# First conditioning rows of a two-layer encoder: plain fp32 products, or split operands in two fp32r passes

## The chip, the cores and the metric

The kernel runs on one core of one Trainium2 chip. The metric is the device time of one execution in microseconds (us). Single executions vary, so the time of a kernel is the median of several runs; beside it stands one execution recorded by the hardware profiler.

A core has TensorE (matmul; its weight loads are listed apart), VectorE, ScalarE, GpSimd and SyncE. SyncE's queue (SP) issues the transfers between DRAM and on-chip memory. Matmuls write into eight PSUM banks of 128 x 512 fp32.

## The reference

A trunk of two layers, for a prompt of 2048 frames and 32 sample frames, width 1024. Each layer scales and shifts its normalised input by rows that come from a conditioning vector:

```python
def ada_norm(x, c, g, w_ada, b_ada):
    mod = jax.nn.silu(c) @ w_ada + b_ada
    shift, scale, gate = jnp.split(mod[:, None, :], 3, axis=-1)
    return rms_norm(x, g) * (1 + scale) + shift, gate

for i in range(DEPTH):
    h_p, gate_p = ada_norm(y_p, c_prompt, norm_g[i], ada_w[i], ada_b[i])
    h_s, gate_s = ada_norm(y_s, c_sample, norm_g[i], ada_w[i], ada_b[i])
    # layer 0: chunk-band attention with a relative bias; layer 1: latent attention
    ...
    y_p = y_p + gate_p * out_p
    y_s = y_s + gate_s * out_s
```

`c` is a vector of 1024 for the prompt and one for the sample; `w_ada` is 1024 x 3072 fp32. The case concerns `shift` and `scale` of layer 0, the first two thirds of `mod`, for both vectors.

## The kernel before

The kernel opens with a prelude: constants, then the conditioning rows of layer 0 (`ada`), then the bias tables and the first 512 frames. Layer 0 follows in 32 steps (two halves, eight pairs of heads, two blocks of 512 frames), then its output projection with the inputs of layer 1, the latent attention, and the end. Nearly all large products run as "split" products: an operand is written as a high part in fp32r and a low part (the rest, also fp32r), and three fp32r matmuls take the place of one in plain fp32. A kernel-wide helper makes the parts: `halve` (L146) casts the raw fp32 tile to the high part on ScalarE (L148) and subtracts that from the raw tile in place on VectorE or GpSimd (L149). `twin` gives a second name with the other type to the same place in memory.

**The conditioning rows before.** `cT` holds silu(c) for both vectors, as eight pieces of 128 x 2. `ada(0, (0, 1), pre[0:11])` (L377) works through two pairs: pair 0 is `shift`, pair 1 `scale`, each 1024 columns. `pre` is a list of sixteen places of 128 x 1024 fp32, which later hold the h tiles `HT0` and `HT1`; in the profile the first eight are called `HT_@1` and the others `HT_@5`. Two places take the bias rows, one takes the finished rows, and a ring of eight takes weight rows. `ada_part` (L272) loads, for each of the eight values of k, 128 rows of `ada_w` (512 KB), and multiplies `cT[:, k]` with their two halves of 512 columns in plain fp32 (L278). VectorE then adds the bias (L282), TensorE turns each piece of 128 columns into a column by a transpose (L291), and VectorE writes `sc` (shift, L298) or `gc` (1 + scale, times the norm's gain, L300).

A weight row can be loaded into a place when the matmuls of the row before it there are done. All transfers are issued from SP's queue (L104), in an order that a scheduler fixes when the program is built: an instruction that is not ready in its reckoning is passed by others. Each engine then runs its queue strictly in order.

**The other conditioning rows** (the gate of layer 0, all of layer 1) are computed during the steps, in `ada_piece` (L304). They use `cH` (L229), where c stands as high part in columns 0 and 1 and low part in columns 2 and 3, and weights split by `halve`; a matmul with the high and one with the low half of the weights (L320) give four rows. `fold` (L232), three identity matrices of 2 x 2 below each other, adds the high rows, the low rows and the bias rows, and turns them to columns at once (L336).

**What comes next in the prelude.** The bias table of layer 0 is loaded, extended by VectorE (L386, L388) and written to DRAM twice (`ext`, `rext`). `make_h` (L415) loads x for 128 frames, takes the mean square on ScalarE in two halves (L344; the squares themselves go to a PSUM bank that nobody reads), normalises (L348), transposes (L428), applies `gc` and `sc` on ScalarE (L432) and splits the result into `HT0` (L435, L436). The banks of tag `tp` and `mx` are three in this part, used in turn by the transposes of `ada` and by these squares. `fetch_w` and `split_w` load and split the projection weights (`wr` to `wq`, casts at L458), and `project` multiplies (L189 to L191, the three matmuls of a split product).

Of the kernel before, what the change touches and what calls it, by code (L numbers as in the profile page):

```python
# [11 lines left out]
ALU = mybir.AluOpType  # L12
# [4 lines left out]
D = 1024  # L17
SEQ = 2048
NS = 32
KT = D // 128  # L20
# [11 lines left out]
def f32(ap):  # L32
    return ap if ap.dtype == F32 else ap.bitcast(F32)
# [49 lines left out]
def located(nc, name, n, dtype, col):  # L83
    t = nc.alloc_sbuf_tensor_at(f"{name}@{len(PLACES)}", [128, n], dtype, offset=BASE + 4 * col).ap()
    PLACES[t.tensor.name] = name, n, dtype, col
    return t


def twin(nc, ap):

    name, n, dtype, col = PLACES[ap.tensor.name]
    key = ap.tensor.name, "twin"
    if key not in PLACES:
        t = PLACES[key] = located(nc, name + "_", n, F32R if dtype == F32 else F32, col)
        PLACES[t.tensor.name, "twin"] = ap
    return bass.AP(PLACES[key].tensor, ap.offset, [list(x) for x in ap.ap])
# [3 lines left out]
def trunk(ctx: ExitStack, tc: tile.TileContext, I, O, stop=99):  # L100
    nc = tc.nc
    V, S, G, T = nc.vector, nc.scalar, nc.gpsimd, nc.tensor
    def dma(dst, src, eng=nc.sync):
        eng.dma_start(f32(dst), f32(src))  # L104
# [21 lines left out]
    ident = const.tile([128, 128], F32, name="ident")  # L126
# [9 lines left out]
    def slot():  # L136
        return wp.tile([128, 2, 512], F32R, tag="w", name="w", bufs=wn)
# [8 lines left out]
    def halve(hi, raw, eng=None):  # L146

        S.copy(hi, raw)  # L148
        (eng or V).tensor_tensor(twin(nc, raw), raw, f32(hi), ALU.subtract)  # L149
# [43 lines left out]
    def bank(tag):  # L193
        order = psum[tag if tag in psum else "mx"]
        order.append(order.pop(0))
        return banks[order[-1]]
# [22 lines left out]
    cT = const.tile([128, KT, 2], F32, name="cT")  # L219
# [9 lines left out]
    cH = const.tile([128, KT, 4], F32R, name="cH")  # L229
    V.tensor_copy(cH[:, :, 0:2], cT)  # L230
    V.tensor_tensor(cH[:, :, 2:4], cT, f32(cH[:, :, 0:2]), ALU.subtract)
    fold = const.tile([6, 2], F32, name="fold")  # L232
# [3 lines left out]
    gate_d = [dram.tile([2, D], F32, name=f"gate{i}") for i in range(2)]  # L236
    gcol, scol = [], []

    def ada(i, parts, ring=None):

        if 0 in parts:
            ada_cols(i)
        gc, sc, gn = gcol[i], scol[i], gnorm[i]

        def row():
            if ring is None:
                return f32(slot()).rearrange("p a b -> p (a b)")
            ring.append(ring.pop(0))
            return ring[-1]

        bias_rows = []
        for pair in parts:
            bias_rows.append(row()[0:2, :])
            dma(bias_rows[-1], bass.AP(I["ada_b"].tensor, I["ada_b"].offset + (3 * i + pair) * D, [[0, 2], [1, D]]))
        modr = row()[0:2, :]
        if ring is not None:
            ring = ring[0:-len(parts) - 1]
        for pair, b in zip(parts, bias_rows):
            ada_part(i, pair, row, gc, sc, gn, b, modr)

    gnorm = []

    def ada_cols(i):
        gn = const.tile([128, KT], F32, name=f"gn{i}")
        dma(gn, I["norm_g"][i].rearrange("(k p) -> p k", p=128))
        gc = const.tile([128, KT, 2], F32, name=f"gc{i}")
        sc = const.tile([128, KT, 2], F32, name=f"sc{i}")
        gcol.append(gc)
        scol.append(sc)
        gnorm.append(gn)  # L270

    def ada_part(i, pair, row, gc, sc, gn, adab, modr):  # L272
        acc = [bank("mm") for _ in range(2)]
        for k in range(KT):
            w = row()
            dma(w, I["ada_w"][i, 128 * k:128 * k + 128, 1024 * pair:1024 * pair + 1024])
            for n in range(2):
                T.matmul(acc[n][0:2, :], cT[:, k, :], w[:, 512 * n:512 * n + 512],  # L278
                         start=(k == 0), stop=(k == KT - 1))
        for n in range(2):  # L280
            mr = modr[:, 512 * n:512 * n + 512]
            V.tensor_tensor(mr, acc[n][0:2, :], adab[:, 512 * n:512 * n + 512], ALU.add)  # L282
            ada_use(i, pair, n, mr)

    def ada_use(i, pair, n, mr):
        if pair == 2:
            dma(gate_d[i][:, 512 * n:512 * n + 512], mr)
            return
        tp = bank("tp")
        for q in range(4):  # L290
            T.transpose(tp[:, 2 * q:2 * q + 2], mr[:, 128 * q:128 * q + 128], ident[0:2, 0:2])  # L291
        ada_cols_use(i, pair, n, tp)

    def ada_cols_use(i, pair, n, tp):
        src = tp[:, 0:8].rearrange("p (k c) -> p k c", c=2)
        ks = slice(4 * n, 4 * n + 4)
        if pair == 0:
            V.tensor_copy(scol[i][:, ks, :], src)  # L298
        else:
            V.scalar_tensor_tensor(gcol[i][:, ks, :], src, 1.0,  # L300
                                   gnorm[i][:, ks].unsqueeze(2).broadcast_to([128, 4, 2]),
                                   ALU.add, ALU.mult)

    def ada_piece(i, pair, n, a, ws, rows):  # L304


        c0 = 1024 * pair + 512 * n
        if a == 0:
            dma(rows[4:6, :], bass.AP(I["ada_b"].tensor, I["ada_b"].offset + 3 * i * D + c0, [[0, 2], [1, 512]]))
        for k in range(2):  # L310
            r0 = 256 * a + 128 * k
            dma(twin(nc, ws[k][1]), I["ada_w"][i, r0:r0 + 128, c0:c0 + 512])
        yield
        for k in range(2):
            halve(ws[k][0], twin(nc, ws[k][1]), G)
        yield
        acc = bank("ad")[0:4, :]
        for k in range(2):
            for x in range(2):
                T.matmul(acc, cH[:, 2 * a + k, :], ws[k][x], start=(k == 0 and x == 0), stop=(k == 1 and x == 1))  # L320
        if a == 0:
            V.tensor_copy(rows[0:4, :], acc)
        else:
            V.tensor_tensor(rows[0:4, :], acc, rows[0:4, :], ALU.add)
        if a < 3:
            return
        if pair == 2:
            out = bank("ad")[0:2, :]
            T.matmul(out, fold, rows, start=True, stop=True)
            t = at1([128, 4, 128], "hs").rearrange("p j t -> p (j t)")[0:2, :]  # L330
            V.tensor_copy(t, out)
            dma(gate_d[i][:, c0 - 2048:c0 - 1536], t)
            return
        tp = bank("tp")
        for q in range(4):
            T.matmul(tp[:, 2 * q:2 * q + 2], rows[:, 128 * q:128 * q + 128], fold, start=True, stop=True)  # L336
        ada_cols_use(i, pair, n, tp)

    def xnorm(x, rows=128):

# [30 lines left out]
    def at1(shape, name, dt=F32, bufs=1):  # L371
        return at.tile(shape, dt, tag=name, name=name, bufs=bufs)


    pre = [twin(nc, at1([128, KT, 1024], f"HT{b}", F32R)) for b in range(2)]
    pre = [t[:, i, :] for t in pre for i in range(KT)]
    ada(0, (0, 1), pre[0:11])  # L377

# [31 lines left out]
    def xraw():  # L412
        return at1([128, D], "xr", bufs=2)
# [555 lines left out]
    for si, s in enumerate(steps):  # L969
# [21 lines left out]
        if si == ADA0:  # L991
            ada_cols(1)
            ring = [[twin(nc, t)[:, 512 * n:512 * n + 512] for n in range(2)] for t in (xraw(), xraw())]
            rows = twin(nc, hsT).rearrange("p k t -> p (k t)")[0:6, :]
            pieces = [ada_piece(i, pair, n, a, ring, rows) for i, pair in ((0, 2), (1, 0), (1, 1), (1, 2))
                      for n in range(2) for a in range(4)]
# [28 lines left out]
        for i, (h, n, c, t) in enumerate(items):  # L1025
# [3 lines left out]
            if len(fifo) > LAGA:  # L1029
                x = fifo.pop(0)  # L1030
# [139 lines left out]
    for t in range(17):  # L1170
        if t < 16:
            for n in range(2):
                out_tile(W, ready[t], n, gp)
            x = ready[t][0]
# [51 lines left out]
    def et(shape, name, dt=F32, bufs=1):  # L1226
        return ep.tile(shape, dt, tag=name, name=name, bufs=bufs)
# [531 lines left out]
    for i in range(len(items) + LAG + 20):  # L1759
# [12 lines left out]
        if i >= LAG and fifo:  # L1772
            u, t, p = fifo.pop(0)
            values(u, t, p)
            if t == u["order"][-1]:
                evac(u)
                later.append((i + DEN, denom, u))
                if u["blk"] % 2 and u["hd"] % 2:
                    n, u0 = INV if u["hd"] < 15 else (7, 9, 10, 10, 11), units[u["i"] - 1]
# [3 lines left out]
        while later and later[0][0] <= i:  # L1783
            _, f, u = later.pop(0)
            f(u)
        if i >= 100 and i % 25 == 0 and wload:
            k, n = wload.pop(0)
# [144 lines left out]
    def row(name):  # L1932
        return et([NS, D], name)
# [62 lines left out]
```

## Time and profile before

| | us |
|---|---|
| median of 3 runs | 3744.6 |
| lowest, highest | 3741.33, 3757.91 |
| the profiled execution | 3754.29 |
| its span in the trace | 3752.5 |

| engine | busy us | share of the span |
|---|---|---|
| TensorE (PE) | 3511.9 | 94% |
| VectorE (DVE) | 2914.7 | 78% |
| ScalarE (ACT) | 2173.0 | 58% |
| GpSimd (POOL) | 1681.1 | 45% |

All moments below are microseconds from the start of the span. Matmul ends are modelled, and matmuls are pipelined, so a matmul's own duration is longer than the distance to the next one; the pace is read from starts. Register, semaphore and transfer-issuing instructions are not counted as busy. The granted clock is TensorE's, as a share of 2.4 GHz.

### The profile page before, as it was taken

The numbers are of one execution on the slowest core, as the hardware profiler recorded it, in microseconds if no ns is written. First come the engines' busy times: TensorE is split into PE (matmuls) and PEld (weight loads), VectorE is DVE, ScalarE is ACT, GpSimd is POOL, SyncE is SP. The second block draws the span as 40 slices with busy tenths as digits, with TensorE's granted clock in tenths as the row PEclk, the third lists the DMA queues.
The fourth block names the chain that finished last, engine by engine and source line by source line (L and its number), as shares of the span: only waits on it lengthen the run. The fifth ranks groups of instructions, "written<-read, shape, count | busy, mean of one in ns | idle before, by whom it ended". The sixth has DMA issues, their size and how long they took to land. (4 is left out here: it accounts for less than half of the span.)

```text
span 3752.5 us, 57503 instructions
## 1 busy us (share of the span) xinstructions
PE 3511.9 (94%) x17834; PEld 2871.1 (77%) x17834; DVE 2914.7 (78%) x6716; ACT 2173.0 (58%) x5302; POOL 1681.1 (45%) x1744
## 2 busy tenths in 40 slices
PE   7899999989999999899989999888999999998999
PEld 4778877867777777677878888767777787777887
DVE  4788888888888888776776766788888888885653
ACT  3556555676666666542223655556776677775542
POOL 0122222344544444340012444458888888884032
PEclk9899999999999999699999999979999999999999
DMA  5222222222333333363444666563233233223253
GB/s 175 69 60 59 69 62 75 81 76 82 99 96 92 96 92 96 96 190 126 132 152 149 181 203 185 171 186 90 74 84 98 67 93 92 68 77 111 89 189 118
DMA packets 441984, 412.91 MB, mean 110 GB/s; under 512 B 68820, under 2 KB 364296, under 8 KB 434636
## 3 DMA queue, kind: packets, MB, share of 16 engines
q1 hardware_dynamic: 441676, 409.23, 37.3%
q8 instruction: 141, 2.31, 0.3%
q14 instruction: 167, 1.37, 0.1%
HBM read 251.72 MB, written 140.10 MB: 104 GB/s over the span
## 5 line engine op out<-in xcount | busy, mean ns | idle before, releaser
L1544 DVE TENSOR_REDUCE mp@325_17580<-bank 128x1 f32<-128x512 f32 (+3 forms) x384 | 233.8, 615 | 28.3 <-PE bank L1543 26.3
L675 ACT ACTIVATE bank<-bank 128x512 f32<-128x512 f32 x448 | 200.3, 447 | 0.0
L678 POOL TENSOR_TENSOR acc@61_865<-acc@61_865,P@63_893 128x256 f32<-128x256 f32 (+3 forms) x64 | 52.9, 826 | 172.4 <-ACT P@63_893 L673 143.3
L1544 DVE TENSOR_REDUCE mp@326_17581<-bank 128x1 f32<-128x512 f32 (+1 forms) x192 | 116.9, 613 | 16.7 <-PE bank L1543 16.0
L1577 ACT ACTIVATE P@436_22812<-bank 128x512 f32<-128x512 f32 (+2 forms) x156 | 83.3, 534 | 74.3 <-issue 38.6
L1577 ACT ACTIVATE P@438_22814<-bank 128x512 f32<-128x512 f32 (+2 forms) x156 | 83.2, 534 | 67.3 <-issue 35.7
L718 DVE RECIPROCAL ez@69_1265<-ez@69_1265 128x128 f32<-128x128 f32 x128 | 117.6, 926 | 0.0
L1577 ACT ACTIVATE P@437_22813<-bank 128x512 f32<-128x512 f32 (+2 forms) x156 | 83.5, 535 | 55.3 <-PE bank L1570 11.3
L1577 ACT ACTIVATE P@435_22811<-bank 128x512 f32<-128x512 f32 (+2 forms) x156 | 83.4, 535 | 54.3 <-issue 13.0
L678 POOL TENSOR_TENSOR acc@61_865<-acc@61_865,P@64_894 128x256 f32<-128x256 f32 (+3 forms) x64 | 53.2, 831 | 114.9 <-ACT P@64_894 L673 92.4
L678 POOL TENSOR_TENSOR acc@62_866<-acc@62_866,P@65_895 128x256 f32<-128x256 f32 (+3 forms) x64 | 53.9, 841 | 106.3 <-ACT P@65_895 L673 103.0
L678 POOL TENSOR_TENSOR acc@62_866<-acc@62_866,P@63_893 128x128 f32<-128x128 f32 (+3 forms) x64 | 54.1, 846 | 103.1 <-ACT P@63_893 L673 96.0
L673 ACT ACTIVATE P@64_894<-bank 128x256 f32<-128x256 f32 (+3 forms) x128 | 52.3, 409 | 76.9 <-DVE bank L667 42.1
L678 POOL TENSOR_TENSOR acc@61_865<-acc@61_865,P@65_895 128x128 f32<-128x128 f32 (+3 forms) x64 | 53.6, 838 | 95.3 <-ACT P@65_895 L673 77.5
L673 ACT ACTIVATE P@63_893<-bank 128x384 f32<-128x384 f32 (+3 forms) x128 | 52.6, 411 | 75.1 <-DVE bank L667 42.7
L673 ACT ACTIVATE P@65_895<-bank 128x128 f32<-128x128 f32 (+3 forms) x128 | 52.4, 409 | 75.0 <-DVE bank L667 44.3
L678 POOL TENSOR_TENSOR acc@62_866<-acc@62_866,P@64_894 128x256 f32<-128x256 f32 (+3 forms) x64 | 54.4, 850 | 86.9 <-ACT P@64_894 L673 84.9
L149 POOL TENSOR_TENSOR ozl@175_14851<-ozl_@180_14859,ozh@173_14849 128x1024 fp32r<-128x1024 f32 x8 | 19.3, 2412 | 151.0 <-ACT ozh@173_14849 L148 151.0
L676 DVE TENSOR_TENSOR Pl@58_862<-bank,Ph@55_859 128x512 fp32r<-128x512 f32 (+3 forms) x150 | 71.3, 475 | 18.1 <-ACT bank L675 16.4
L676 DVE TENSOR_TENSOR Pl@60_864<-bank,Ph@57_861 128x384 fp32r<-128x384 f32 (+3 forms) x149 | 71.7, 481 | 11.6 <-ACT bank L675 9.3
L676 DVE TENSOR_TENSOR Pl@59_863<-bank,Ph@56_860 128x384 fp32r<-128x384 f32 (+3 forms) x149 | 72.7, 488 | 8.3 <-ACT bank L675 5.8
L1594 DVE TENSOR_TENSOR bank<-bank,P@437_22813 128x512 f32<-128x512 f32 (+2 forms) x108 | 66.5, 616 | 12.8 <-ACT P@437_22813 L1577 12.0
(2154 smaller groups left out, 14849.6 us busy)
## 6 DMA issues: line engine op xcount, KB each, us to landing
h<-hT@203_14883 SPq DMA_DIRECT2D x16, 1024.0 KB
N<-hl@389_17976 SPq DMA_DIRECT2D x32, 512.0 KB
N<-hl@390_17977 SPq DMA_DIRECT2D x32, 512.0 KB
wr@10_296<-in_a_w_in SPq DMA_DIRECT2D x64, 192.0 KB
wr@11_297<-in_a_w_in SPq DMA_DIRECT2D x64, 192.0 KB
xr@9_231<-in_ada_w SPq DMA_DIRECT2D x32, 256.0 KB
xr@8_230<-in_ada_w SPq DMA_DIRECT2D x32, 256.0 KB
h1@220_14902<-h SPq DMA_DIRECT2D x8, 1024.0 KB
```

The source lines that it names most:

```text
L149: (eng or V).tensor_tensor(twin(nc, raw), raw, f32(hi), ALU.subtract)
L673: S.activation(P[:, 0:w], st[:, 0:w], AF.Exp)
L675: S.activation(st[:, 0:w], st[:, 0:w], AF.Exp)
L676: V.tensor_tensor(Pl[:, 0:w], st[:, 0:w], f32(Ph[:, 0:w]), ALU.subtract)
L678: G.tensor_tensor(u["acc"][:, qs], u["acc"][:, qs], P[:, 0:w], ALU.add)
L718: V.reciprocal(ez[:, cs], ez[:, cs])
L1544: V.tensor_reduce(mp[:, j, c:c + 1] if blk else m4[:, j:j + 1], X[:, 0:w], AX.X, ALU.max)
L1577: S.activation(P[:, 0:w], st[:, 0:w], AF.Exp)
L1594: V.tensor_tensor((u["acc"] if last else u["sum"])[:, qs], old, P[:, 0:w], ALU.add)
```

## The change

The first conditioning rows are computed in the manner of `ada_piece`, but by whole weight rows:

- `cH` takes the place of `cT` as the stationary operand, so a product has four rows.
- Ten places of `pre` are used, not eleven. Two hold the rows of the two pairs (four product rows and two bias rows each); the other eight are four pairs of places, one for the high and one for the low part of a weight row. The raw row is loaded into the low part's place.
- `halve` casts each 128 x 1024 row on ScalarE and subtracts on VectorE.
- For each half of 512 columns TensorE multiplies with the high and with the low part, in fp32r: four matmuls for each row in place of two plain fp32 products.
- The PSUM rows are copied by VectorE, and `fold` adds the six rows and turns them to columns.
- The bias rows of a pair are loaded at the start of that pair; before, both were loaded ahead of all weight rows.

`ada_use` is now shared by both ways. Nothing else of the program is changed.

```diff
-    def ada(i, parts, ring=None):
...
+    def ada(i, parts, ring):
+
+        ada_cols(i)
+        places = [(twin(nc, ring[2 + 2 * j]), twin(nc, ring[3 + 2 * j])) for j in range(4)]
         for pair in parts:
-            bias_rows.append(row()[0:2, :])
-            dma(bias_rows[-1], bass.AP(I["ada_b"].tensor, I["ada_b"].offset + (3 * i + pair) * D, [[0, 2], [1, D]]))
-        modr = row()[0:2, :]
-        if ring is not None:
-            ring = ring[0:-len(parts) - 1]
-        for pair, b in zip(parts, bias_rows):
-            ada_part(i, pair, row, gc, sc, gn, b, modr)
+            rows = ring[pair][0:6, :]
+            dma(rows[4:6, :], bass.AP(I["ada_b"].tensor, I["ada_b"].offset + (3 * i + pair) * D, [[0, 2], [1, D]]))
+            acc = [bank("mm")[0:4, :] for _ in range(2)]
+            for k in range(KT):
+                hi, lo = places[(KT * parts.index(pair) + k) % 4]
+                dma(twin(nc, lo), I["ada_w"][i, 128 * k:128 * k + 128, 1024 * pair:1024 * pair + 1024])
+                halve(hi, twin(nc, lo))
+                for n in range(2):
+                    for x in (hi, lo):
+                        T.matmul(acc[n], cH[:, k, :], x[:, 512 * n:512 * n + 512], start=(k == 0 and x is hi),
+                                 stop=(k == KT - 1 and x is lo))
+            for n in range(2):
+                half = rows[:, 512 * n:512 * n + 512]
+                V.tensor_copy(half[0:4, :], acc[n])
+                ada_use(i, pair, n, half)
...
-    def ada_part(i, pair, row, gc, sc, gn, adab, modr):
-        acc = [bank("mm") for _ in range(2)]
-        for k in range(KT):
-            w = row()
-            dma(w, I["ada_w"][i, 128 * k:128 * k + 128, 1024 * pair:1024 * pair + 1024])
-            for n in range(2):
-                T.matmul(acc[n][0:2, :], cT[:, k, :], w[:, 512 * n:512 * n + 512],
-                         start=(k == 0), stop=(k == KT - 1))
-        for n in range(2):
-            mr = modr[:, 512 * n:512 * n + 512]
-            V.tensor_tensor(mr, acc[n][0:2, :], adab[:, 512 * n:512 * n + 512], ALU.add)
-            ada_use(i, pair, n, mr)
...
+    def ada_use(i, pair, n, rows):
+
         tp = bank("tp")
         for q in range(4):
-            T.transpose(tp[:, 2 * q:2 * q + 2], mr[:, 128 * q:128 * q + 128], ident[0:2, 0:2])
-        ada_cols_use(i, pair, n, tp)
...
+            T.matmul(tp[:, 2 * q:2 * q + 2], rows[:, 128 * q:128 * q + 128], fold, start=True, stop=True)
...
-    ada(0, (0, 1), pre[0:11])
+    ada(0, (0, 1), pre[0:10])
```

## Rows read from the trace of the kernel before

**Rows 1.** The page's first part: busy us, share of the span and instructions of each engine.

```profile
PE 3511.9 (94%) x17834; PEld 2871.1 (77%) x17834; DVE 2914.7 (78%) x6716; ACT 2173.0 (58%) x5302; POOL 1681.1 (45%) x1744
```

**Rows 2.** Busy time of each engine in three stretches, and a heading line.

```profile
core 0: us, PE busy (x) PEld busy (x) DVE busy (x) ACT busy (x) POOL busy (x), PEclk, DMA share, GB/s
7.30:39.30 32.00, 31.50 (x80) 6.71 (x80) 4.48 (x11) 1.07 (x3) 0.00 (x0) 1.00 0.86 313
39.30:48.30 9.00, 3.41 (x18) 2.79 (x17) 7.58 (x31) 7.96 (x30) 0.00 (x0) 0.81 0.60 160
65.00:1400.00 1335.00, 1254.73 (x6486) 1026.08 (x6487) 1106.14 (x2903) 841.67 (x2124) 479.21 (x507) 0.98 0.28 78
```

**Rows 3.** Line L278: durations in ns (min/median/max), first and last start, shapes.

```profile
L278 PE MATMUL bank<-HT_@1_125,cT x40: 591/592/1061, 7.4 to 32.4; 128*2 128x512 f32 x40
...
L278 PE MATMUL bank<-HT_@5_127,cT x24: 592/592/592, 18.2 to 37.5; 128*2 128x512 f32 x24
```

**Rows 4.** Timeline of the weight loads: start, duration, form, idle before and what ended it.

```profile
9.01 0.13 PEld L278 LDWEIGHTS bank<-HT_@1_125,cT 128*2 128x2 f32 x1 [0.72 <-issue]
...
16.47 0.09 PEld L278 LDWEIGHTS bank<-HT_@1_125,cT 128*2 128x2 f32 x1 [0.34 <-issue]
```

**Rows 5.** SP's queue in the timeline (issue of transfers), and a stretch at full rate.

```profile
3.43 0.84 SPq L104 DMA_DIRECT2D HT_@1_125<-in_ada_w  x2
4.32 1.96 SPq L104 DMA_DIRECT2D fold<-ident  x3
...
23.52 0.33 SPq L104 DMA_DIRECT2D HT_@5_127<-in_ada_w  x1
23.95 0.38 SPq L104 DMA_DIRECT2D HT_@5_127<-in_a_rel_bias  x1
...
30.73 0.42 SPq L104 DMA_DIRECT2D xr@8_230<-in_x_prompt  x1
...
12.00:17.00 5.00, 5.00 (x13) 1.02 (x12) 0.00 (x0) 0.00 (x0) 0.00 (x0) 1.00 1.02 415
```

**Rows 6.** Waits of SP's queue, 0 to 80 us: total, times, longest.

```profile
SPq L104 <- PE bank L278: 11.3, 8, 1.9
```

**Rows 7.** Timeline from the last product to the first projection matmul, three engines.

```profile
36.59 0.60 ACT L344 ACTIVATE bank<-xr@8_230 128x512 f32<-128x512 f32 x1 [32.04 <-DMA xr@8_230<-in_x_prompt]
37.31 0.68 DVE L282 TENSOR_TENSOR HT_@1_125<-bank,HT_@1_125 2x512 f32<-2x512 f32 x1 [7.19 <-PE bank L278]
38.77 0.14 DVE L300 SCALAR_TENSOR_TENSOR gc<-bank,gn 128x8 f32<-128x8 f32 x1
38.95 0.60 ACT L344 ACTIVATE bank<-xr@8_230 128x512 f32<-128x512 f32 x1 [1.63 <-DVE gc L300]
43.81 0.49 ACT L458 CAST wq@12_300<-wr@10_296 128x384 fp32r<-128x384 f32 x1
45.77 1.51 ACT L432 ACTIVATE hs@20_334<-bank,sc,gc 128x128 f32<-128x128 f32 x4
48.29 0.44 PE L189 MATMUL bank<-wq@12_300,HT0@0_124 128*128 128x384 f32 x1 [0.30 <-DVE HT0@0_124 L435]
```

**Rows 8.** The later conditioning pieces: fp32r matmuls and fold in the timeline, copy by line.

```profile
906.30 0.63 PE L320 MATMUL bank<-xr_@76_8239,cH 128*4 128x512 f32 x2
906.77 0.40 PE L320 MATMUL bank<-xr_@79_8240,cH 128*4 128x512 f32 x1
...
1084.45 1.05 PE L336 MATMUL bank<-fold,hsT_@82_8241 6*128 6x2 f32 x8
...
L322 DVE COPY hsT_@82_8241<-bank x8: 616/670/678, 910.9 to 1363.6; 4x512 f32<-4x512 f32 x8
```

**Rows 9.** The helper's cast and subtraction of 128x1024 elsewhere, by line, in ns.

```profile
L148 ACT CAST vh@140_14377<-vraw@116_14156 x4: 1045/1046/1048, 1508.6 to 1589.1; 128x1024 fp32r<-128x1024 f32 x4
...
L149 DVE TENSOR_TENSOR vraw_@141_14379<-vraw@116_14156,vh@140_14377 x4: 1199/1214/1247, 1522.0 to 1593.0; 128x1024 fp32r<-128x1024 f32 x4
```

**Rows 10.** One load of 512 KB and the cast that waits for it, in the timeline.

```profile
3607.62 0.38 SPq L104 DMA_DIRECT2D cv_@549_33007<-in_cache_mla_ckv  x1
...
3611.71 1.05 ACT L148 CAST cv@547_33005<-cv_@549_33007 128x1024 fp32r<-128x1024 f32 x1 [2.46 <-DMA cv_@549_33007<-in_cache_mla_ckv]
```

More of the change, by code (lines that the diff above doesn't have):

```diff
@@ L237, in trunk @@
     gcol, scol = [], []
-    def ada(i, parts, ring=None):
[L241 to L251, printed above, removed]
-        for pair in parts:
-            bias_rows.append(row()[0:2, :])
-            dma(bias_rows[-1], bass.AP(I["ada_b"].tensor, I["ada_b"].offset + (3 * i + pair) * D, [[0, 2], [1, D]]))
-        modr = row()[0:2, :]
-        if ring is not None:
-            ring = ring[0:-len(parts) - 1]
-        for pair, b in zip(parts, bias_rows):
-            ada_part(i, pair, row, gc, sc, gn, b, modr)
+    def ada(i, parts, ring):
+        ada_cols(i)
+        places = [(twin(nc, ring[2 + 2 * j]), twin(nc, ring[3 + 2 * j])) for j in range(4)]
+        for pair in parts:
+            rows = ring[pair][0:6, :]
[13 more added lines that the diff above has]
+                ada_use(i, pair, n, half)
     gnorm = []
@@ L270, in ada_cols @@
         gnorm.append(gn)
-    def ada_part(i, pair, row, gc, sc, gn, adab, modr):
-        acc = [bank("mm") for _ in range(2)]
-        for k in range(KT):
-            w = row()
-            dma(w, I["ada_w"][i, 128 * k:128 * k + 128, 1024 * pair:1024 * pair + 1024])
-            for n in range(2):
-                T.matmul(acc[n][0:2, :], cT[:, k, :], w[:, 512 * n:512 * n + 512],
-                         start=(k == 0), stop=(k == KT - 1))
-        for n in range(2):
-            mr = modr[:, 512 * n:512 * n + 512]
-            V.tensor_tensor(mr, acc[n][0:2, :], adab[:, 512 * n:512 * n + 512], ALU.add)
-            ada_use(i, pair, n, mr)
[L285 to L288, printed above, removed]
+    def ada_use(i, pair, n, rows):
         tp = bank("tp")
         for q in range(4):
-            T.transpose(tp[:, 2 * q:2 * q + 2], mr[:, 128 * q:128 * q + 128], ident[0:2, 0:2])
-        ada_cols_use(i, pair, n, tp)
-    def ada_cols_use(i, pair, n, tp):
+            T.matmul(tp[:, 2 * q:2 * q + 2], rows[:, 128 * q:128 * q + 128], fold, start=True, stop=True)
         src = tp[:, 0:8].rearrange("p (k c) -> p k c", c=2)
@@ L333, in ada_piece @@
             return
[L334 to L337, printed above, removed]
+        ada_use(i, pair, n, rows)
     def xnorm(x, rows=128):
```

## The prediction

> **What bounds the kernel now.** I began with the page's engine shares: TensorE is busy for 94% of the span [rows 1], so whatever delays the start of its long stream delays the end by as much. Then came the busy time by stretch, for the place where the change lies. From 7.3 to 39.3 us TensorE is busy for 31.5 of 32.0 us with the conditioning rows; from 39.3 to 48.3 us it is busy for 3.4 of 9.0 us, while ScalarE is busy for 8.0; from 65 us on it runs at 94% (1254.7 of 1335.0) [rows 2]. The change touches the first of these stretches only, and everything behind it waits for the end of that stretch. The whole stretch is under 1% of the kernel, so no outcome of it can be large. What matters is when the first projection matmul starts: 48.29 us [rows 7].
>
> Inside the prelude I read the weight loads of TensorE for the pace, the SP queue for the transfers, and the moments at which the three engines hand on. The 32 products of 512 columns in plain fp32 stand in the trace as 64 matmuls, 40 + 24 [rows 3]. The first ones follow each other by 0.72 + 0.13 = 0.85 us, the later ones by 0.34 + 0.09 = 0.43 us [rows 4]: the 1.2 GHz level first, then 2.4 GHz (the profile's granted clock says 1.00 for the whole stretch [rows 2]). So TensorE, not the transfers, is the bound: 16 rows of 512 KB are 8.39 MB, which at the 415 GB/s of 12 to 17 us [rows 5] is 20.2 us. The queue shows the same from its side: SP waited 11.3 us, in 8 waits, for TensorE to give a row's place back [rows 6].
>
> **What the change removes and adds.** Removed: 64 matmuls of 0.43 us, 27.5 us at full clock and some 30 as they ran. Added: 64 fp32r matmuls of 512 columns. Two of them take 0.63 us where one takes 0.40 in the later conditioning pieces [rows 8], so they follow each other by 0.23 us: 64 x 0.23 = 14.7 us. Per weight row there is also one ScalarE cast, 1.05 us, and one VectorE subtraction, 1.21 us, for 128x1024 (rows of the same helper and shape) [rows 9]: 16.8 and 19.4 us in all, on engines that have nothing else to do there, ScalarE before 36.59 us [rows 7]. The bias add becomes a PSUM copy of 0.67 us, and the four small transposes become eight small matmuls, 1.05 us together [rows 8].
>
> By busy time no engine and no queue would need more than some 20 us, and the stretch should shrink by 10 us. That is not the sum I make, because the places decide. Before, eight rows could be on their way. Now there are four pairs of places, and a place is given back only after transfer, cast, subtraction and the last product with the low half. One turn of a place:
> - transfer of 512 KB, alone: issued at 3607.62, used at 3611.71 us, so 4.1 us [rows 10];
> - cast 1.05, subtraction 1.21;
> - three matmuls behind the subtraction, 3 x 0.23 = 0.7 (the first needs only the high half).
>
> That is 7.1 us. Four places give one row per 1.8 us, above the 1.21 us of VectorE and the 1.3 us of a row's transfer at full rate. The first row is usable at about 7.35 us, as now (issue 3.43 plus 3.9) [rows 5], and is done at some 10.9 with cold matmuls. Rows 5, 9 and 13 end three turns later, at 32.2; rows 14 to 16 follow at VectorE's pace, 3 x 1.26, giving 36.0. The change of pairs on the two accumulators costs some 0.5. So the last product ends at 36.5 us if nothing else uses the transfers. Now it ends about when the add starts, 37.31 us [rows 7]. A halved matmul buys under 1 us.
>
> The tail behind it: copy 0.67, eight matmuls 1.05, the column operation 0.14 and hand-overs, 2.1 us to the first L300, against 38.77 - 37.31 = 1.46 now [rows 7]. So the first L300 would start at 38.6 us, level with 38.77 now.
>
> **What is late next.** The squares of the first x tiles share the PSUM banks with the conditioning columns: the second square starts at 38.95, right behind the L300 at 38.77 [rows 7]. So ScalarE's chain (seven squares, four casts of the projection weights from 43.81, the first h from 45.77, projection at 48.29) hangs on the L300: 9.5 us behind it, now and after. The second thing that it needs is x. Its load is issued at 30.73, 7.2 us behind the last weight row (23.52), because the small transfers and the bias tables stand between, and it is usable at 36.59 [rows 5, 7]. In the new kernel the last weight row is issued when row 12 frees its place, about 29.4 us. Two orders of the queue are possible:
> - **x stays behind all weight rows.** Its chain moves by 29.4 - 23.5 = 5.9 us: usable at 42.5, second square 43.2 instead of 38.95. The projection starts 4.2 us later.
> - **x is moved ahead**, into the time in which SP waits for a place. The order is not the program's: the three loads of fold stand first in the code, and SP issues two weight rows before them [rows 5]. With a wait of some 4 us behind the fourth row I think this likelier, 3 to 1. Then four x tiles, 2.1 MB or 5.1 us at 415 GB/s, mix with the weight rows. The bandwidth is shared, so they lengthen the turns; 20.2 + 5.1 us fit into the 30, but only where the gaps are. I bound this at 0 and 6 us and take half, 3 us: first L300 at 41.6, 2.8 us later than now.
>
> Against this stand the four weight casts at 43.81 to 45.77, 2.0 us [rows 7]. Their loads could come forward as well, and the casts would then run in the gaps before the L300. Credit 0 to 2 us; I take none, because ScalarE's queue is in order and the rows' own casts stand there.
>
> Forecast: both orders land 3 to 4 us late. **The projection starts 3.5 us later, and the end moves with it**: 3752.5 becomes 3756 for the span, and the profiled execution's 3754.3 becomes 3757.8. This execution was 9.7 us above the median of the three, so on the median's scale the result is 3744.6 + 3.5 = **3748 us**.
>
> The Trainium skill, "DMA: Bandwidth & Descriptors", section "Anatomy of one DMA", prices a transfer at a fixed 2.0 us plus its bytes at 436 GB/s, a fit for another way of issuing. For 512 KB that is an estimate of 3.2 us, against 4.1 measured here; by it a turn would be 6.2 us, and the last product would end nearer 34 us. The trace decides, and I keep 4.1.
>
> **Rivals.**
> - **It comes out a little faster (3742 us).** The loads fit the gaps (0 instead of 3) and the four casts come forward (2.0 us); a turn shared by fewer transfers takes 3.9 us of load, as the first row does, which gives 0.6 over three turns. With the 0.2 us by which the bare sum lies below before that is 2.8 us. For it speaks the idle of ScalarE and VectorE; against it, the in-order queues.
> - **TensorE runs at the lower clock (3753 us).** It now waits for every row: 4 x 0.23 = 0.9 us of work in 1.8. Where it was busy for 3.4 of 9.0 us, the granted clock was 0.81 [rows 2], so waits lower it here; at what share they do, no row shows. At 1.2 GHz a matmul takes 0.43, the four of a row 1.7 us, and the turn 0.6 more, with TensorE itself near the pace: the end moves to some 41.5, and with shared transfers to 46. With the tail of 2.1 the L300 comes at 43.6 to 48.1, 5 to 9 us later than now; I take 8. The Trainium skill says the same in "TensorE: Matmul & The Clock Gate", section "HAM oscillation": matmul groups that wait for a transfer between them fall back to the lower clock.
> - **The turns fall in line (slower, 3767 us).** If SP's queue holds a transfer that must wait (a bias table behind its DRAM write, a second projection weight behind its cast) ahead of the weight rows, the four places turn two by two: 3.6 us per row instead of 1.8, some 16 to 22 us more. This decides only if the wait stands ahead of most rows from the fifth on; now SP's waits in the prelude are short, 11.3 us over 8 [rows 6].
> - **The rest shifts.** Operations, banks and places behind the prelude are the same, but the order of the queues is made anew; I have no row that prices this, and give it 5 us either way.
>
> **How the numbers follow.** Forecast 0.55, faster rival 0.20, lower clock 0.17, turns in line 0.05, the rest 0.03. A measurement of this kernel tells about 0.5%, 19 us, from no change. Of the cases only the third rival reaches that, and the runs of before themselves spread over 17 us. So faster 0.02, same 0.92, slower 0.06. Range: 3742 less 5 for the spread of a median, to 3753 plus 8 for the same and the upper end of the second rival: 3737 to 3761.
>
> **What would show it.** In the changed kernel: the casts of the weight rows at a mean pitch near 1.8 us, with ScalarE idle for transfers between them; the fifth weight row issued near 11, the last near 30 us; the first L300 between 39 and 44 and the first projection matmul 9 to 10 us behind it. Wrong if weight rows come at 1.3 us (then it gains about 8 us), if the squares no longer wait for L300, or if the end doesn't move with the start.

## The result, and the profile after

The changed kernel takes 3809.6 us (median of 4 runs, 3802.3 to 3817.2); the kernel before, run beside it, takes 3743.0 (4 runs, 3738.6 to 3757.9). The ratio is 1.0163 with a 95% interval of [1.0144, 1.0181], which is some 61 us (54 to 68; the medians lie 66.6 apart), where the forecast was 3 to 4 us and the range ended at 3761. The profiled executions took 3802.3 and 3754.3 us, 48 us apart: the one of after is the fastest of its four, the one of before is 11 us above its median.

The page's first part, with the columns of [rows 1]:

```profile
PE 3507.3 (92%) x17850; PEld 2865.3 (75%) x17850; DVE 2937.8 (77%) x6732; ACT 2189.2 (58%) x5318; POOL 1679.9 (44%) x1744
```

No engine has much more to do: TensorE has 4.6 us less, VectorE 23 and ScalarE 16 more, near the 19.4 and 16.8 us that the prediction gave to the subtractions and casts of the sixteen rows. The time went into waiting. Busy time by stretch, with the columns of [rows 2]:

```profile
7.30:92.70 85.40, 31.82 (x79) 6.02 (x80) 26.67 (x33) 22.58 (x30) 0.00 (x0) 0.67 0.45 135
92.70:103.00 10.30, 6.34 (x33) 5.14 (x32) 8.34 (x31) 6.51 (x24) 0.00 (x0) 0.67 0.40 119
119.80:1400.00 1280.20, 1196.88 (x6193) 979.75 (x6194) 1056.84 (x2767) 802.76 (x2028) 450.78 (x478) 0.98 0.28 78
```

The stretch with the conditioning rows lasts 85.4 us in place of 32.0. TensorE is busy for 31.8 of them, the transfers move 135 GB/s where they moved 313 [rows 2], and no engine is near full. From 119.8 us on TensorE is busy for 93.5% at a granted clock of 0.98, much as before (94.0%, 0.98). One step of this stretch, from the timeline of SP, ScalarE, VectorE and TensorE (start, duration, operation; in brackets the idle time before it and what ended that), and the same cast in three later steps:

```profile
10.45 0.33 SPq L104 DMA_DIRECT2D HT_@1_125<-in_ada_w  x1
...
13.96 1.04 ACT L148 CAST HT0@0_124<-HT_@1_125 128x1024 fp32r<-128x1024 f32 x1 [4.65 <-DMA HT_@1_125<-in_ada_w]
...
15.04 1.23 DVE L149 TENSOR_TENSOR HT0@0_124<-HT_@1_125,HT0@0_124 128x1024 fp32r<-128x1024 f32 x1 [0.74 <-ACT HT0@0_124 L148]
15.05 1.01 PE L253 MATMUL bank<-HT0@0_124,cH 128*4 128x512 f32 x2 [4.64 <-ACT HT0@0_124 L148]
16.32 1.01 PE L253 MATMUL bank<-HT0@0_124,cH 128*4 128x512 f32 x2 [0.25 <-DVE HT0@0_124 L149]
17.36 0.34 SPq L104 DMA_DIRECT2D HT_@1_125<-in_ada_w  x1
...
67.55 1.04 ACT L148 CAST HT0@0_124<-HT_@1_125 128x1024 fp32r<-128x1024 f32 x1 [6.07 <-DMA HT_@1_125<-in_ada_w]
...
74.54 1.04 ACT L148 CAST HT0@0_124<-HT_@1_125 128x1024 fp32r<-128x1024 f32 x1 [5.95 <-DMA HT_@1_125<-in_ada_w]
...
81.42 1.04 ACT L148 CAST HT0@0_124<-HT_@1_125 128x1024 fp32r<-128x1024 f32 x1 [3.02 <-DMA HT_@1_125<-in_ada_w]
```

Load, cast, subtraction, last product, and only then the next load: 17.36 - 10.45 = 6.9 us. It is the turn of a place as the forecast summed it (7.1), but no other turn of `HT0` runs beside it. The casts by line, and what SP's queue waited for from 0 to 100 us (total, times, longest):

```profile
L148 ACT CAST HT0@0_124<-HT_@1_125 x12: 1027/1044/1045, 7.0 to 88.4; 128x1024 fp32r<-128x1024 f32 x12
L148 ACT CAST HT1@4_126<-HT_@5_127 x4: 1041/1044/1045, 8.3 to 77.4; 128x1024 fp32r<-128x1024 f32 x4
```

```profile
SPq L104 <- DVE HT0@0_124 L149: 36.8, 9, 5.6
SPq L104 <- PE bank L253: 21.5, 14, 8.4
```

Twelve of the sixteen rows lie in `HT0`, three of the four pairs of places; their casts go from 7.0 to 88.4 us, 11 intervals of 6.8 to 10.0 with a mean of 7.4. SP waits 58.3 us for VectorE and TensorE, where it waited 11.3 [rows 6]. From there the delay is handed on, from the timeline, which begins with SP's queue:

```profile
63.84 7.44 SPq L104 DMA_DIRECT2D HT_@1_125<-in_ada_w  x2
72.65 0.33 SPq L104 DMA_DIRECT2D HT_@5_127<-in_ada_w  x1
77.94 7.21 SPq L104 DMA_DIRECT2D HT_@1_125<-in_ada_w  x2
93.55 0.80 SPq L104 DMA_DIRECT2D HT_@5_127<-in_x_prompt  x2
94.88 0.17 DVE L281 SCALAR_TENSOR_TENSOR gc<-bank,gn 128x8 f32<-128x8 f32 x1 [0.65 <-PE bank L275]
...
103.26 0.67 PE L189 MATMUL bank<-wq@12_364,HT0@0_124 128*128 128x384 f32 x1
```

`gc` comes at 94.88 in place of 38.77, and the first projection matmul 8.4 us behind it, at 103.26 in place of 48.29 [rows 7]: 55.0 us later. The span of the two profiled executions is 47.8 longer and the ratio says 61, so the start carries the change, to within some 7 us.

### The profile page after: what moved, and what is told of

It reads as the page before. It is cut to its first block, busy times and chain, and to the rows that moved or that the text cites. A ratio compares the mean times of both kernels' runs of the same rounds, so it can differ in the third digit from the quotient of the medians.

```text
span 3800.3 us, 57611 instructions
## 1 busy us (share of the span) xinstructions
PE 3507.3 (92%) x17850; PEld 2865.3 (75%) x17850; DVE 2937.8 (77%) x6732; ACT 2189.2 (58%) x5318; POOL 1679.9 (44%) x1744
## 5 line engine op out<-in xcount | busy, mean ns | idle before, releaser
L1522 DVE TENSOR_REDUCE mp@326_17645<-bank 128x1 f32<-128x512 f32 (+1 forms) x192 | 117.2, 614 | 16.8 <-PE bank L1521 16.4
L651 ACT ACTIVATE P@63_957<-bank 128x384 f32<-128x384 f32 (+3 forms) x128 | 52.5, 410 | 74.0 <-DVE bank L645 41.6
L253 PE MATMUL bank<-HT0@0_124,cH 128*4 128x512 f32 x48 | 24.0, 599 | 60.9 <-ACT HT0@0_124 L148 57.5
```

The costliest lines, as they stand in the source:

```text
L253: T.matmul(acc[n], cH[:, k, :], x[:, 512 * n:512 * n + 512], start=(k == 0 and x is hi), stop=(k == KT - 1 and x is lo))
L651: S.activation(P[:, 0:w], st[:, 0:w], AF.Exp)
L1522: V.tensor_reduce(mp[:, j, c:c + 1] if blk else m4[:, j:j + 1], X[:, 0:w], AX.X, ALU.max)
```

## The experiments

**The theory.** A weight row is loaded under one name of its place (the fp32 name that `twin` gives, `HT_@1` in the trace) and its two parts are written and read by the products under the other (`HT0`, fp32r). Waits within one name are made slice by slice; between the two names of one place they are made for the whole tensor. So each load into any of the three pairs in `HT0` waits until the row before it in `HT0` is done with, and the three pairs act as one.

**The rivals.** Something else spreads the rows: the order of SP's queue (the third rival of the prediction), the clock, four places being too few at a turn of 7 us, or a new order of the whole program. Each run below is timed beside the kernel before on the same chip. With each ratio stands the moment of the first projection matmul, which is read from one profiled execution of each kernel (48.29 before, [rows 7]).

**A name for each place.** Every one of the sixteen places becomes a tensor of its own at the same address, with its own second name. Operations, sizes, places and the program's order stay.

```diff
-    pre = [twin(nc, at1([128, KT, 1024], f"HT{b}", F32R)) for b in range(2)]
-    pre = [t[:, i, :] for t in pre for i in range(KT)]
+    pre = [PLACES[at1([128, KT, 1024], f"HT{b}", F32R).tensor.name][3] for b in range(2)]
+    pre = [located(nc, f"pre{b}", 1024, F32, c + 1024 * i) for b, c in enumerate(pre) for i in range(KT)]
```

> The changed kernel, but each of the sixteen places is a tensor of its own at the same address, with its own twin, in place of sixteen slices of two large tensors. Theory (a wait between the two names of one place is made for the whole tensor, so the three pairs inside HT0 turn one after the other, 12 rows at 7.0 us): now four places turn at once, rows come every 1.8 to 2.2 us, the last product ends at 36 to 43 us instead of 92.5, the first projection matmul starts at 46 to 54 us instead of 103.3, and the time is 3743 to 3752 us. Rival (SP's queue in order, with other loads ahead of the weight rows, makes the rows wait): the same loads are in the queue, so rows still come at about 5.5 us and the time stays near 3810. Rival (four places are too few, whatever the names): the last product ends at 60 us or later, 3770 us or more.

Measured: 3765.7 us, ratio 1.0047 [1.0034, 1.0061]; first projection matmul at 56.09. The expectation, 46 to 54 us and a time of 3743 to 3752, was missed by 2 and 14 us. SP's queue and the end of the prelude from the timeline, the stretch, and two of the four groups of casts by line:

```profile
27.00 0.33 SPq L104 DMA_DIRECT2D pre0@5_129<-in_ada_w  x1
28.70 0.33 SPq L104 DMA_DIRECT2D pre0@7_131<-in_ada_w  x1
30.41 0.33 SPq L104 DMA_DIRECT2D pre0@9_133<-in_ada_w  x1
32.09 0.33 SPq L104 DMA_DIRECT2D pre1@11_135<-in_ada_w  x1
...
40.16 1.85 SPq L104 DMA_DIRECT2D xr@42_316<-in_x_prompt  x1
41.50 0.17 DVE L281 SCALAR_TENSOR_TENSOR gc<-bank,gn 128x8 f32<-128x8 f32 x1 [0.54 <-PE bank L275]
45.90 0.60 ACT L322 ACTIVATE bank<-xr@42_316 128x512 f32<-128x512 f32 x1 [8.34 <-DMA xr@42_316<-in_x_prompt]
...
56.09 0.69 PE L189 MATMUL bank<-wq@46_386,HT0@0_124 128*128 128x384 f32 x1
```

```profile
7.30:39.00 31.70, 22.72 (x78) 6.49 (x78) 21.23 (x21) 16.47 (x16) 0.00 (x0) 0.89 0.71 238
```

```profile
L148 ACT CAST pre_@18_146<-pre0@5_129 x4: 1044/1044/1045, 7.0 to 30.6; 128x1024 fp32r<-128x1024 f32 x4
...
L148 ACT CAST pre_@36_152<-pre1@11_135 x4: 1045/1046/1047, 10.8 to 36.5; 128x1024 fp32r<-128x1024 f32 x4
```

The sixteen casts go from 7.0 to 36.5 us, a mean pitch of 1.96, and the last four rows are issued every 1.70: near the pace that the prediction made from four places (1.8). The stretch falls back from 85 to 32 us, and of the 55.0 us by which the first projection matmul was late, 47.2 are gone. The cause of those is shown. What stays, 7.8 us, is x: its load stands behind all the weight rows again (40.16, against 30.73 in [rows 5]), and the first square waits for it until 45.90.

**The same names in the kernel before**, with the plain fp32 products as they were (the same two lines).

> The kernel before with the same sixteen tensors of their own. It writes and reads its weight rows under one name only. Theory (whole-tensor waits arise only between two names of one address): nothing changes in the prelude, last product at about 37 us, time within 0.3% of before. Rival (own tensors are better or worse by themselves, for example by the order that the scheduler makes of them): the time moves by more than 0.3%, and then the gain of the other run is not the names' alone.

Measured: 3749.7, ratio 1.0008 [0.9994, 1.0021].

```profile
47.38 0.69 PE L189 MATMUL bank<-wq@22_314,HT0@0_124 128*128 128x384 f32 x1
```

The projection starts 0.9 us earlier than before, and the time doesn't change, as expected. Before, the rows were loaded and read under one name, so there was nothing to part.

**Two pairs in each tensor.** If the tensor is what couples them, four pairs spread two and two over `HT0` and `HT1` should turn two rows at a time.

```diff
-    ada(0, (0, 1), pre[0:10])
+    ada(0, (0, 1), pre[0:6] + pre[8:12])
```

> The changed kernel with two pairs of places inside HT0 and two inside HT1, instead of three and one. Theory: two chains of eight rows at 7.0 us each go side by side, 8 x 7.0 = 56 us, so the last product ends at about 60 to 63 us instead of 92.5 and the time falls by about 30 us against the changed kernel, to about 3780. Rival (queue order, or too few places): four pairs as before, no change, 3810 us.

Measured: 3803.1, ratio 1.0142 [1.0115, 1.0169], first projection matmul at 99.79. The expectation, some 3780 us, missed by 23. The timeline of SP's queue says why:

```profile
28.10 0.34 SPq L104 DMA_DIRECT2D HT_@5_127<-in_ada_w  x1
29.80 0.34 SPq L104 DMA_DIRECT2D HT_@1_125<-in_ada_w  x1
...
39.98 0.35 SPq L104 DMA_DIRECT2D HT_@5_127<-in_ada_w  x1
40.39 0.42 SPq L104 DMA_DIRECT2D HT_@1_125<-in_ada_w  x1
```

This list takes the pairs in the order `HT0`, `HT0`, `HT1`, `HT1`. SP issues the rows in that order, so only the rows at a seam go out together (28.10 and 29.80, 39.98 and 40.39); the second row of a tensor holds up the queue for a whole turn. I had counted places and not their order.

**The same two and two, taken in turn.** The order is now `HT0`, `HT1`, `HT0`, `HT1`.

```diff
-    ada(0, (0, 1), pre[0:10])
+    ada(0, (0, 1), pre[0:4] + pre[8:10] + pre[4:6] + pre[10:12])
```

> The changed kernel with the four pairs taken from HT0 and HT1 in turn (first and third in HT0, second and fourth in HT1); the run with two and two had them in the order HT0, HT0, HT1, HT1, and TensorE and SP take rows strictly in order, so there only rows at the seam between the two tensors could overlap. Theory (a row waits for every use of the other name of its whole tensor): each tensor holds one row at a time, neighbours are always in different tensors, so two rows turn together: eight rounds of 7 to 8 us and some 6 us for the loads that SP has among them, last product at 65 to 72 us instead of 92.5, about 24 us less than the changed kernel, near 3785. Rival (the number of rows at a time does not depend on the tensor): no change from the run with two and two, near 3800.

Measured: 3786.4, ratio 1.0094 [1.008, 1.0108]: as expected. Four successive casts of weight rows, and the projection:

```profile
56.62 1.04 ACT L148 CAST HT0@0_124<-HT_@1_125 128x1024 fp32r<-128x1024 f32 x1 [2.60 <-DMA HT_@1_125<-in_ada_w]
59.80 1.04 ACT L148 CAST HT1@4_126<-HT_@5_127 128x1024 fp32r<-128x1024 f32 x1 [2.13 <-DMA HT_@5_127<-in_ada_w]
63.64 1.04 ACT L148 CAST HT0@0_124<-HT_@1_125 128x1024 fp32r<-128x1024 f32 x1 [2.80 <-DMA HT_@1_125<-in_ada_w]
66.84 1.04 ACT L148 CAST HT1@4_126<-HT_@5_127 128x1024 fp32r<-128x1024 f32 x1 [2.16 <-DMA HT_@5_127<-in_ada_w]
...
81.19 0.67 PE L189 MATMUL bank<-wq@12_364,HT0@0_124 128*128 128x384 f32 x1
```

Each tensor still has one turn of 7.0 us (56.62 to 63.64, 59.80 to 66.84), and two run side by side: a row per 3.5 us. There are four pairs of places as in the changed kernel, and two lines of turns decide.

**Four places for the weight rows, in the kernel before.** This separates the number of places from the names: plain fp32 products, one name, and a ring of four rows where there were eight.

```diff
-    ada(0, (0, 1), pre[0:11])
+    ada(0, (0, 1), pre[0:7])
```

> The kernel before, with a ring of four weight places instead of eight. One name, so the slices should be kept apart. Theory: a turn is 4.1 us of transfer and 1.7 us of four fp32 matmuls, 5.8 us, over four places 1.45 us per row, under the 1.72 us of TensorE per row; the last product ends within 3 us of 37, time within 0.2% of before. Rival (four places are too few, or slices of one tensor are never kept apart): rows come at 1.9 us or more, or one by one at 5.8 us, and the time rises by 5 us, or by 55 us.

Measured: 3753.5, ratio 1.0015 [1.0002, 1.0028], within the 0.2% expected.

```profile
39.53 0.14 DVE L300 SCALAR_TENSOR_TENSOR gc<-bank,gn 128x8 f32<-128x8 f32 x1
...
42.49 0.60 ACT L344 ACTIVATE bank<-xr@8_230 128x512 f32<-128x512 f32 x1 [37.89 <-DMA xr@8_230<-in_x_prompt]
...
52.52 0.69 PE L189 MATMUL bank<-wq@12_300,HT0@0_124 128*128 128x384 f32 x1
```

The rows are hardly later: `gc` comes at 39.53, 0.8 us behind before. Four places alone put the projection 4.2 us later, again because x stands behind the weight rows (first square at 42.49, against 36.59 in [rows 7]). So four slices of one tensor do turn side by side as long as they are loaded and read under one name.

**Eight pairs, each its own tensor.** Three of the pairs lie in a part of memory that is free during the prelude.

```diff
-        places = [(twin(nc, ring[2 + 2 * j]), twin(nc, ring[3 + 2 * j])) for j in range(4)]
+        places = [(twin(nc, ring[2 + 2 * j]), twin(nc, ring[3 + 2 * j])) for j in range(8)]
...
-                hi, lo = places[(KT * parts.index(pair) + k) % 4]
+                hi, lo = places[(KT * parts.index(pair) + k) % 8]
...
-    ada(0, (0, 1), pre[0:10])
...
+    pre = [located(nc, f"pre{b}", 1024, F32, c + 1024 * i) for b, c in enumerate(pre) for i in range(KT)]
+    pre[12:12] = [located(nc, "pre2", 1024, F32, 43728 + 1024 * i) for i in range(8)]
+    ada(0, (0, 1), pre[0:18])
+    del pre[12:20]
```

> The changed kernel with places that are tensors of their own, and eight pairs of them instead of four. Theory (with four pairs of their own a turn of 7.1 us over four places sets the pace, as the prediction said): eight places bring the pace down to that of the transfers or of VectorE, 1.2 to 1.3 us per row; last product at 28 to 32 us instead of 39. The x tiles stay behind the weight rows in SP's queue, issued at about 30 us, usable at 36, the first projection matmul at 45 to 48 us instead of 56.1, so 8 to 11 us less than with four pairs, within 0.2% of before. Rival (TensorE at its lower clock, or VectorE, sets the pace): last product at 36 us or later, no gain from eight.

Measured: 3759.2, ratio 1.0028 [1.0009, 1.0047]. From the timeline and the busy time by stretch:

```profile
18.70 1.05 ACT L148 CAST pre_@32_156<-pre0@7_131 128x1024 fp32r<-128x1024 f32 x1 [0.23 <-DMA pre0@7_131<-in_ada_w]
19.98 1.04 ACT L148 CAST pre_@38_158<-pre0@9_133 128x1024 fp32r<-128x1024 f32 x1 [0.23 <-DMA pre0@9_133<-in_ada_w]
...
33.65 0.17 DVE L281 SCALAR_TENSOR_TENSOR gc<-bank,gn 128x8 f32<-128x8 f32 x1 [0.54 <-PE bank L275]
...
47.56 0.69 PE L189 MATMUL bank<-wq@78_402,HT0@0_124 128*128 128x384 f32 x1
```

```profile
7.30:32.00 24.70, 21.55 (x80) 7.18 (x80) 21.65 (x23) 16.63 (x16) 0.00 (x0) 0.93 0.78 307
```

With places enough, a row comes every 1.28 us, close to the pace of the subtraction (1.21, [rows 9]) and of the transfers, and `gc` is there at 33.65, 5.1 us earlier than before. That is what the split products can bring. But the projection gains 0.7 us only: the first square of x waits for its load until 36.58, as before (36.59, [rows 7]), so the faster rows run into the wait for x. In the time nothing of a gain is left, and here the expectation, within 0.2% of before, missed. The profiled execution, 3743.4 us, is the fastest of ten with a median of 3759.2.

**x ahead of the second half of the rows.** To take that wait away, the loads of the first x tiles and of two projection weights go between `shift` and `scale`, and the bias tables behind both; the squares of the first block use a bank of another tag, so that they no longer wait for `gc`. With the eight pairs of the run before:

```diff
         for pair in parts:
+            if pair == parts[-1]:
+                between()
...
-            junk = bank("tp")
+            junk = bank(tag)
...
+    def between():
+        for m in first:
+            next(m)
+        for c in range(2):
+            fetch_w(0, c)
+
+    ada(0, (0, 1), ring, between)
+    rext_d = dram.tile([AH, EXT], F32, name="rext")
```

> Eight pairs of places of their own; the x tiles and two projection weights are loaded between the two pairs of conditioning rows, the bias tables after them, and the first squares write to a bank that the conditioning columns don't use. Theory (what then ends last is the scale column itself): weight rows end with the transfers, 8.4 + 2.9 MB at 0.41 MB per us from 5.5 us on, 33 us; last product 36, first L300-kind column 38 to 39, first projection matmul 41 to 43 us, 5 to 7 us before 48.3; time 0.1 to 0.25% under before. Rival (ScalarE's queue, with casts of rows, squares and casts of weights in one order, ends last): first projection matmul at 46 us or later, no gain.

Measured: 3751.0, ratio 0.9997 [0.9988, 1.0006].

```profile
41.18 0.17 DVE L283 SCALAR_TENSOR_TENSOR gc<-bank,gn 128x8 f32<-128x8 f32 x1 [0.54 <-PE bank L277]
...
44.68 0.60 PE L189 MATMUL bank<-wq@78_404,HT0@0_124 128*128 128x384 f32 x1
```

Now x waits for `gc`: the projection follows 3.5 us behind it in place of 9.5, and starts 3.6 us earlier than before. But `gc` itself is at 41.18 again, 7.5 us later than with the rows in one piece, because the rows of `scale` come behind x and the weights (issued from 18.42 to 24.09), and their casts stand behind the squares and the weights' casts in ScalarE's queue (the first at 26.58). VectorE, which subtracts, is busy without a gap from 27.6 to 39.0 as well; which of the two costs more is not shown. In the time that is no difference from before, which again falls short of what was expected (a start at 41 to 43 us, a time 0.1 to 0.25% lower).

**The same order in the kernel before**, with plain fp32 products, the ring of eight and the one name: the edit above without the split products.

> The kernel before, fp32 products and its ring of eight, with the same order of loads and the same bank for the squares as the run before this one. Theory (TensorE sets the pace of fp32 rows at 1.72 us, and the second eight rows now come behind x): last product at 38 to 40 us, first projection matmul at 42 to 44 us; time 0.05 to 0.2% under before, and the split rows add only 1 to 3 us to that. Rival (the gain is the split's): no change from before, 48 us.

Measured: 3743.9, ratio 0.9981 [0.9972, 0.999].

```profile
44.51 0.14 DVE L302 SCALAR_TENSOR_TENSOR gc<-bank,gn 128x8 f32<-128x8 f32 x1
...
46.71 0.44 PE L189 MATMUL bank<-wq@12_302,HT0@0_124 128*128 128x384 f32 x1
```

The projection starts 1.6 us earlier, and the time falls by some 7 us [3.7, 10.5]. It is the only version that lies clearly below the kernel before, though by less than the 0.5% that the prediction set as the bound, and 5 of the 7 us are more than its start explains. The expectation had the start at 42 to 44 us and the split rows 1 to 3 us ahead in the time. The start missed by 3 us; the split rows start the projection 2.0 us earlier than this run, and in the time they are some 6 us behind it. So with the loads in this order the split products bring nothing more.

**All runs together.** The shift of the first projection matmul and the change in time by the ratio, both against before, in us:

| | start of the projection | time |
|---|---|---|
| the change | +55.0 | +61 |
| two and two in blocks | +51.5 | +53 |
| two and two in turn | +32.9 | +35 |
| own names | +7.8 | +18 |
| eight pairs | -0.7 | +10 |
| before, ring of four | +4.2 | +6 |
| before, own names | -0.9 | +3 |
| split, x early | -3.6 | -1 |
| before, x early | -1.6 | -7 |

The large shifts go over into the time nearly one to one. With the small ones, -5 to +11 us remain beside the start. In the traces of all of them the queues hold, from some 116 us at the latest, the same work in the same order as before, so a new order of the program isn't the reason; no run settles what is. One thing goes with it: from run to run of one kernel the time follows the granted clock over the whole span. With eight pairs it was 0.967 in the run of 3743 us and 0.958 in that of 3777. For the last row of the table its median is 0.968, against 0.965 for the runs of before beside it, so part of those 7 us may be the clock's and not the order's.

## Why the prediction was wrong

- **The bound was read rightly.** Everything waits for the first projection matmul, and its 55 us became the loss. "No outcome of it can be large" was wrong: the stretch was under 1% of the kernel, but nothing keeps a stretch from growing.
- **The turn of a place was right**: 7.1 us forecast, 6.9 measured in the step shown (load 3.51, cast 1.08, subtraction 1.28, last matmuls 1.04, as distances between starts). The load was 0.6 cheaper than summed and the matmuls 0.3 dearer. The estimate from the Trainium skill's fit, which is for another way of issuing ("DMA: Bandwidth & Descriptors", "Anatomy of one DMA"), is 3.2 us and lies below these 3.5 as well, though nearer than the 4.1 that I took.
- **The step that failed: "Four places give one row per 1.8 us."** I divided a turn by the number of places without asking whether they turn independently. The diff shows the answer: each row is loaded into `twin(nc, lo)` and read as `lo`, and `twin` had been applied to all of `HT0`. With names of their own the four places gave one row per 1.96 us in the mean; with the order in turn, two lines gave one per 3.5; as the change stood, three pairs in one line gave one of their rows per 7.4 in the mean (6.8 to 10.0). The 16 rows lasted till 93 in place of 36.5.
- **Where the places are parted, the rest of the sum is some 3 us short.** With own names x stood behind all weight rows, the first of the two orders of the queue, for which the sum has `gc` at 38.6. It came at 41.50; that this is near the 41.6 of the other order, with shared transfers, is chance. The term that was too small is the change of pairs, put at 0.5 us: VectorE's copies and `sc` stand there between two subtractions, which start 4.5 us apart (20.16 and 24.68) in place of 1.2. The projection was 7.8 us late in place of 4.2, because the last row went out at 32.09 and not at 29.4, and x after it at 40.16.
- **x was moved ahead in the changed kernel**, as thought likelier: its first two tiles are issued at 12.02 and 12.49, the first projection weights at 12.97. It was worth nothing, since the rows ended so late. The other two x tiles lie in `HT1` and were caught by the same coupling: 93.55, after the last product of the rows.
- **"TensorE runs at the lower clock" came true and decided nothing.** The granted clock was 0.67 over the stretch, and two matmuls took 1.01 us where they take 0.63 at the high level [rows 8]. That agrees with the Trainium skill, "TensorE: Matmul & The Clock Gate", "HAM oscillation", by which matmul groups that wait for a transfer between them fall back to the lower clock. Where the rows came closer together the granted clock was 0.89 (own names) and 0.93 (eight pairs). But four products of 0.43 us are 1.7 us in a turn of 7, half of them beside the subtraction. The rival's price has a slip as well: a turn of 7.7 us three times behind 10.9, three rows at 1.7 and 0.5 for the change of pairs make 39.7 us, not 41.5.
- **"The turns fall in line" had the right shape and the wrong mechanism and price.** I looked for a transfer ahead in SP's queue that must wait, and priced turns two by two at 16 to 22 us. From 64 to 93 us SP issues nothing but weight rows, and the turns are still 7 us. The wait was in the row's own load. At 0.05 and 3767 us, this rival was both too cheap and too unlikely.
- **"The rest shifts"** is excluded as a new order, as said above. A remainder of up to 11 us beside the start is there in several kernels, and its cause is open.

## What to carry over

Before a ring of places is costed as a pipeline, look at how each place is named where it is written and where it is read: if these are two names of one larger tensor, the waits between them are made for the whole of it, as in these runs, and all the places in it turn as one. Give each place a tensor of its own, or at least put neighbours in the ring into different tensors; here that took 47 and 22 us off the start. And where the path forks (here the conditioning columns and x), a faster branch is worth no more than its distance to the other: with split rows 5 us earlier, the projection started 0.7 us earlier.

## What the runs showed of the hardware

Plain fp32 products of few rows were no loss here. The split form needs 0.23 us per matmul at the high clock [rows 8] against 0.43, but a row then depends on a load, a cast and a subtraction in turn, and the granted clock was 0.67 to 0.93 over such stretches where it was 1.00 before [rows 2]. In the run with x early the products that had waited for ScalarE and VectorE started at the slow pace and found the fast one in the middle of the burst; the granted clock was 0.50 from 27.6 to 34.6 us and 0.97 from there to 39.0:

```profile
33.82 1.05 PE L255 MATMUL bank<-pre_@41_163,cH 128*4 128x512 f32 x2
34.67 0.70 PE L255 MATMUL bank<-pre_@44_164,cH 128*4 128x512 f32 x2
35.21 0.62 PE L255 MATMUL bank<-pre_@47_165,cH 128*4 128x512 f32 x2
35.67 0.63 PE L255 MATMUL bank<-pre_@50_166,cH 128*4 128x512 f32 x2
```

From start to start two products take 0.85 us and then 0.47: 0.43 and 0.23 for one, the 1.2 and the 2.4 GHz level. At the low level the split form has no advantage left for a row: four products of 0.43 against four matmuls of 0.43 in the plain form at the high level.
